# Ordering every engine's instructions by the scheduler's timeline model instead of its ordinary one

## The chip, the cores and the metric

The kernel runs on one core of a Trainium2 chip. The metric is device time in microseconds, from one run of the whole program. Times of a profiled execution come from a hardware trace of one run.

## The reference, cut to what matters

One layer of a hybrid mixer. A sequence of 2048 tokens by 1024 channels is normalized and projected, the columns are split over four mixers of width 256, each mixer runs along the sequence, and the joined result is projected back, normalized and added to the input.

```python
h = _rmsnorm(x, pre_norm_w[l])
proj = jnp.einsum('btd,de->bte', h, w_in[l])
p_gdn, p_rwkv, p_sc, p_gla = _split(proj, [GDN_COLS, RWKV_COLS, SC_COLS, GLA_COLS])
y_gdn = _gated_deltanet(...)   # chunks of 64: triangular solve, then a scan over chunks
y_rwkv = _rwkv7(...)           # a scan over tokens
y_sc = _short_conv(...)
y_gla = _gla(...)              # chunks of 64, a scan over chunks
y = jnp.concatenate([y_gdn, y_rwkv, y_sc, y_gla], axis=-1)
out = jnp.einsum('bte,ed->btd', y, w_out[l])
x = x + _rmsnorm(out, post_norm_w[l])
```

Each scan carries a state of 64x64 (GLA: 32x64) per head from chunk to chunk, four heads a mixer. RWKV is computed in chunks too, with a triangular inverse as for the gated delta rule.

## The kernel before

The sequence is cut into 4 blocks of 512 tokens, a block into 4 tiles of 128 tokens, a tile into 2 chunks of 64. All products run on TensorE (PE) through one helper line (L197) and transposes through another (L201), so a row of the profile is told apart by the tile it writes: `pp` are the projections (`proj` L476, `out_proj` L1322), `psi` the triangular inverses (`inverse` L558), `psc` the chains that carry the states (`gdn_chain` L971, `rwkv_chain` L1017, `gla` L1249), `psa` everything else (transposes, chunk matrices). Their PSUM banks are 2, 1, 2 and 3 (BANKS, L169).

Projections are in single precision split into a high and a low part (`hh`, `hl` of the activations, two halves of a tile `w` of the weights), three products each. A weight tile of 128 columns comes in two halves of 12 matmuls of 512 columns; a ring of NW = 3 halves (L161) is loaded ahead. In block 0 `load_parts` (L451) loads raw weights, splits them on ScalarE (ACT) and GpSimd (POOL) (`split`, L348) and stores the parts to DRAM; later blocks load the parts (L465). All DMAs are issued on SyncE's (SP's) queue.

An inverse works on two tiles at once: five doubling levels, each a product on `psi`, a masking on VectorE (DVE; `W`, L591), a second product, an addition (`X`, L596), a transposition and two copies; then a correction. A GDN chunk has three dependent products: state times keys, the solve (`gu<-`), the state update, with DVE or ACT between them. So inverses and chains alternate between PE and another engine, visit by visit. A norm needs a power -1/2, which POOL computes (`power`, L352, at L354).

The source decides the program order itself. Generators for chains (priority 0), inverses (1), preparation (2), outputs (3), row norms (4), late weights (5) and projections (99) are woven by `weave` (L227), which keeps a clock `t` of its own from matmul sizes, and lets projections fill until BEAT = 1.5 us of it have passed before the others get a turn:

```python
ready = [th for th in self.threads if th[0] < 99 and self.can(th)]
if main[0] == 99 and self.can(main) and (not ready or self.t - self.left < BEAT):
    self.step(main)
```

This program order isn't yet the order on the engines. When the TileContext block closes (L1431), the framework's scheduler ranks every instruction by its place in the program (`high_priority` blocks move it up by 400 places, or 4000), plays the program on a model of the chip's engines, and hands each engine of the model, when it can take one, the ready instruction of lowest rank. The lists that result are what the chip's engines run, each in its list's order, with semaphores between them. Buffers are tiles of fixed rings, so the order doesn't change which buffer an instruction uses.

## Time and profile before

| | before |
|---|---|
| median of 3 runs | 1380.93 us (1374.62 to 1382.09) |
| the profiled execution | 1382.66 us, span 1380.9 us |
| mean granted TensorE clock | 0.979 of full speed |
| busy, PE / PEld / DVE / ACT / POOL | 93% / 71% / 70% / 39% / 26% |
| moved by DMA | 204.47 MB, mean 148 GB/s |

PE is the matmul stream and PEld the weight loads, which overlap it. The span runs from the first to the last instruction. An engine's busy time is the time in which at least one of its instructions is recorded as running; a wait is put down to the instruction that released it.

### The profile page before, as it was taken

What the parts mean: (1) busy time and instruction counts of PE and PEld (TensorE: products, weight loads), DVE (VectorE), ACT (ScalarE), POOL (GpSimd) and SP (SyncE); (2) the same over time, 40 slices, a digit from 0 to 9 for tenths busy, and PEclk for the clock granted to TensorE, in tenths of its full rate; (3) what the DMA queues carried; (4) which work ended last, traced back from release to release, by engine and by line L of the source; (5) the groups of instructions that cost most, each with busy time, mean ns of one, the idle gap of its engine ahead of it and who ended that gap; (6) DMA issues with size and microseconds to landing.
All of it is one profiled execution on the core that took longest, in us unless ns stands there. A gap on an engine that the chain in (4) does not pass through costs nothing. (4 is left out here: it accounts for less than half of the span.)

```text
span 1380.9 us, 25696 instructions
## 1 busy us (share of the span) xinstructions
PE 1286.0 (93%) x9928; PEld 974.5 (71%) x9928; DVE 966.9 (70%) x2194; ACT 532.1 (39%) x1165; POOL 357.1 (26%) x437
## 2 busy tenths in 40 slices
PE   5989988899999999999999899999998998999997
PEld 3767766667767777767677677676776776777886
DVE  5776697778886787688757894888669847643222
ACT  4653454235442441435524422453234234232221
POOL 5564443301121121111311211103112144232221
PEclk9999999999999999999999999999999998999999
DMA  7876554453244424453444333532444362233442
GB/s 278 272 253 228 206 176 145 142 167 121 92 139 136 155 93 151 140 177 123 139 145 137 123 126 130 165 125 93 146 134 142 117 213 87 93 111 100 150 151 99
DMA packets 98506, 204.47 MB, mean 148 GB/s; under 512 B 9152, under 2 KB 39248, under 8 KB 98384
## 3 DMA queue, kind: packets, MB, share of 16 engines
q1 hardware_dynamic: 98384, 202.83, 44.6%
q8 instruction: 78, 1.28, 0.4%
q14 instruction: 44, 0.36, 0.1%
HBM read 153.51 MB, written 49.28 MB: 147 GB/s over the span
## 5 line engine op out<-in xcount | busy, mean ns | idle before, releaser
L197 PE MATMUL pp<-hh,w 128*128 128x512 f32 (+1 forms) x2272 | 642.2, 408 | 7.9 <-ACT hh L432 4.0
L197 PEld LDWEIGHTS pp<-hh,w 128*128 128x128 f32 (+1 forms) x2272 | 413.0, 190 | 96.8 <-issue 5.1
L197 PE MATMUL pp<-hl,w 128*128 128x512 f32 (+1 forms) x1152 | 340.7, 408 | 2.0 <-POOL hl L433 2.0
L197 PEld LDWEIGHTS pp<-hl,w 128*128 128x128 f32 (+1 forms) x1152 | 209.3, 190 | 47.3 <-POOL hl L433 3.8
L350 POOL TENSOR_TENSOR w<-raw,w 128x512 fp32r<-128x512 f32 (+1 forms) x102 | 129.2, 1270 | 222.1 <-ACT w L349 121.6
L354 POOL TENSOR_TENSOR sm<-sm,mhalf 128x4 f32<-128x4 f32 (+1 forms) x64 | 59.7, 933 | 221.7 <-DVE sm L1077 196.0
L349 ACT CAST w<-raw 128x512 fp32r<-128x512 f32 (+1 forms) x102 | 60.4, 594 | 132.2 <-issue 60.9
L197 PE MATMUL pp<-woh,w 128*128 128x512 f32 x256 | 73.8, 409 | 0.0
L659 DVE SCALAR_TENSOR_TENSOR pq<-pq,par,pq 128x512 f32<-128x512 f32 x72 | 59.0, 819 | 14.7 <-ACT pq L656 12.3
L583 DVE COPY Yb<-Y 64x512 f16<-64x512 f16 x160 | 57.2, 358 | 2.2
L197 PEld LDWEIGHTS <-Yb 128*128 128x128 f16 x640 | 24.9, 99 | 44.5 <-issue 18.7
L197 PE MATMUL psi<-W,Yb 128*128 128x64 f16 x640 | 33.1, 196 | 23.5 <-DVE W L591 16.9
L197 PEld LDWEIGHTS pp<-woh,w 128*128 128x128 f32 x256 | 48.0, 193 | 9.5
L596 DVE TENSOR_TENSOR X<-psi,X 128x512 f16<-128x512 f32 x64 | 43.9, 686 | 9.6 <-PE psi L197 9.2
L197 PEld LDWEIGHTS <-Bb 128*128 128x128 f16 x768 | 29.6, 99 | 27.2 <-issue 21.6
L1368 DVE SCALAR_TENSOR_TENSOR pq<-pq,sm,x 128x512 f32<-128x512 f32 x32 | 24.0, 751 | 31.1 <-DMA x<-in_x 20.6
L598 DVE STREAM_TRANSPOSE Y<-X 128x512 f16<-128x512 f16 x64 | 45.2, 706 | 0.9
L1357 ACT ACTIVATE x<-pp 128x512 f32<-128x512 f32 x32 | 19.1, 598 | 68.8 <-PE pp L197 68.8
L591 DVE TENSOR_TENSOR W<-psi,c 128x512 f16<-128x512 f32 x64 | 43.6, 682 | 1.7 <-PE psi L197 1.2
L197 PE MATMUL psi<-X,Bb 128*128 128x64 f16 x768 | 39.7, 195 | 4.1 <-DVE X L596 3.6
L994 ACT COPY gu<-psc 64x128 f32<-64x128 f32 x64 | 16.7, 260 | 59.0 <-PE psc L197 58.0
L1358 DVE TENSOR_TENSOR pq<-pp,lg 128x512 f32<-128x512 f32 x16 | 11.1, 691 | 36.2 <-ACT x L1357 36.2
(317 smaller groups left out, 2087.2 us busy)
## 6 DMA issues: line engine op xcount, KB each, us to landing
w<-parts SPq DMA_DIRECT2D x186, 512.0 KB, 3.3
parts<-w SPq DMA_DIRECT2D x62, 512.0 KB, 4.0
raw<-in_wt SPq DMA_DIRECT2D x62, 256.0 KB, 3.1
x<-in_x SPq DMA_DIRECT2D x56, 256.0 KB, 3.0
raw<-yd SPq DMA_DIRECT2D x32, 256.0 KB, 2.9
out<-pq SPq DMA_DIRECT2D x32, 256.0 KB, 2.1
x<-in_xt SPq DMA_DIRECT2D x24, 256.0 KB, 2.9
yd<-y SPq DMA_DIRECT2D x32, 128.0 KB, 2.0
```

The source lines that it names most:

```text
L197: return self.nc.tensor.matmul(out, w, x, **kw)
L349: self.nc.scalar.copy(hi, src)
L350: self.nc.gpsimd.tensor_tensor(lo, src, hi.bitcast(F32), ALU.subtract)
L354: self.nc.gpsimd.tensor_tensor(dst, x, self.mhalf[:, 0:x.shape[1]], ALU.pow)
L583: nc.vector.tensor_copy(Yb[hs(c), :, hs(c)], Y[hs(c)])
L591: nc.vector.tensor_tensor(W, v(ps), m4(self.lev[lv]), ALU.mult)
L596: nc.vector.tensor_tensor(X2, v(ps), X, ALU.add)
L598: nc.vector.transpose(Y, X)
L659: nc.vector.scalar_tensor_tensor(acc, p[:, i:i + BL], self.pcol("conv", 4 * ct + i), acc, ALU.mult, ALU.add)
L994: nc.scalar.copy(qh(w)[q, :, hp, :], pB[hs(hp), 0:P].rearrange("p (q d) -> p q d", q=2))
L1357: nc.scalar.activation(junk, ps[i], AF.Square, accum_out=ss[:, i:i + 1])
L1368: nc.vector.scalar_tensor_tensor(o, o, r, x, ALU.mult, ALU.add)
```

## The change

One argument of the TileContext. The program that is traced, its ranks, its tiles and its priorities are the same; the model on which the scheduler plays it is another. The framework has two models, which it calls CoreSim and TimelineSim, the second being the more detailed. So the order of the instructions on each engine can change, and the order of the DMAs on SP's queue, and nothing else.

```diff
     out = nc.dram_tensor("out_0", (S, D), F32, kind="ExternalOutput").ap()
-    with tile.TileContext(nc) as tc:
+    with tile.TileContext(nc, schedule_with_timeline_sim=True) as tc:
         K(tc, aps, out).build()
```

## Rows read from the trace of the kernel before

**Rows 1.** The page: busy us (share of the span) x instructions.

```profile
PE 1286.0 (93%) x9928; PEld 974.5 (71%) x9928; DVE 966.9 (70%) x2194; ACT 532.1 (39%) x1165; POOL 357.1 (26%) x437
```

**Rows 2.** Windows: busy us of each engine, granted clock, DMA share, GB/s.

```profile
core 0: us, PE busy (x) PEld busy (x) DVE busy (x) ACT busy (x) POOL busy (x), PEclk, DMA share, GB/s
...
595.00:880.00 285.00, 270.38 (x2289) 201.91 (x2287) 218.23 (x521) 111.94 (x249) 48.07 (x74) 1.00 0.43 139
...
0.00:310.00 310.00, 268.67 (x1798) 202.89 (x1799) 225.11 (x450) 143.83 (x293) 134.32 (x146) 0.96 0.60 207
...
310.00:1165.00 855.00, 813.13 (x6872) 611.55 (x6872) 653.78 (x1559) 336.10 (x745) 167.55 (x237) 0.99 0.42 135
...
1165.00:1381.00 216.00, 204.18 (x1260) 160.10 (x1259) 88.05 (x188) 52.18 (x127) 55.23 (x54) 0.97 0.35 116
```

**Rows 3.** Waits of PE: total us, times, longest.

```profile
PE psi L197 <- DVE W L591: 16.9, 11, 4.8
...
PE psa L201 <- POOL gs L354: 12.1, 1, 12.1
...
PE pp L197 <- DMA w<-parts: 2.4, 3, 1.2
```

**Rows 4.** Timeline around one PE stall: start us, us, then the group.

```profile
759.97 1.21 DVE L871 TENSOR_TENSOR_SCAN t<-c,t 128x512 f32<-128x512 f16 x1
...
761.12 0.67 DVE L591 TENSOR_TENSOR W<-psi,c 128x512 f16<-128x512 f32 x1
...
761.85 0.41 PE L197 MATMUL psi<-W,Yb 128*128 128x64 f16 x8 [1.75 <-DVE W L591]
...
762.09 1.39 PE L197 MATMUL pp<-hh,w 128*128 128x512 f32 x5
```

**Rows 5.** Timeline of a GDN chain in block 2.

```profile
706.16 0.60 PE L197 MATMUL psc<-Sg,kq 128*128 128x128 f32 x4
...
707.71 0.42 DVE L984 TENSOR_TENSOR gu<-gu,vT 64x256 f32<-64x256 f32 x1
...
708.52 0.45 PE L197 MATMUL psc<-gu,Yf 64*64 64x64 f32 x8
...
708.90 2.11 PE L197 MATMUL pp<-hh,w 128*128 128x512 f32 x8
...
710.94 0.45 PE L197 MATMUL psc<-gu,kT 64*64 64x64 f32 x8
```

**Rows 6.** Windows of PE alone on pp, psa, psc, psi, in that order.

```profile
595.00:880.00 285.00, 202.58 (x759) 1.00 0.43 139
595.00:880.00 285.00, 39.35 (x410) 1.00 0.43 139
595.00:880.00 285.00, 40.13 (x640) 1.00 0.43 139
595.00:880.00 285.00, 21.05 (x480) 1.00 0.43 139
```

**Rows 7.** Matmuls on psi from 595 to 880 us, two of four forms.

```profile
L197 PE MATMUL psi<-X,Bb x192: 189/193/203, 596.3 to 830.8; 128*128 128x64 f16 x192
...
L197 PE MATMUL psi<-W,Yb x160: 189/193/203, 598.5 to 828.2; 128*128 128x64 f16 x160
```

**Rows 8.** Chain that ended last, its longest step: start us, us, work, count.

```profile
1276.35 97.06 PE pp L197 x428
```

**Rows 9.** POOL's elementwise lines on the page, and a wait of DVE for POOL.

```profile
L350 POOL TENSOR_TENSOR w<-raw,w 128x512 fp32r<-128x512 f32 (+1 forms) x102 | 129.2, 1270 | 222.1 <-ACT w L349 121.6
...
L354 POOL TENSOR_TENSOR sm<-sm,mhalf 128x4 f32<-128x4 f32 (+1 forms) x64 | 59.7, 933 | 221.7 <-DVE sm L1077 196.0
...
DVE lu L1081 <- POOL sm L354: 15.1, 16, 1.9
```

**Rows 10.** SP's queue: what its weight loads wait for.

```profile
SPq L465 <- PE pp L197: 520.5, 150, 15.5
```

**Rows 11.** The page's DMA issues: count, KB each, us to landing.

```profile
raw<-in_wt SPq DMA_DIRECT2D x62, 256.0 KB, 3.1
```

## The prediction

> **What bounds the kernel now.** The page's busy table comes first: TensorE (PE) has 1286.0 us of matmul in a span of 1380.9 [rows 1], so 94.9 us of PE time is idle, and that is all that a new order of the same instructions can give back, unless the instructions themselves become shorter. The profiled execution took 1382.66 us, its span and 1.8 us around it; the median of the three timed runs is 1380.93, so a sum made against 1382.7 stands 1.7 us above the median.
>
> Next the windows show where the idle time lies [rows 2]. The first 310 us (block 0, its weights split for the first time) hold 41 us of it, the steady stretch from 310 to 1165 holds 42, the end 12. The steady stretch is three periods of 285 us, one per block; one of them has 270.4 us of PE work and 14.6 idle. The list of waits says what the idle pieces are: 12.1 us is one wait at the start, for POOL's row scale; the rest are waits of a few us, nearly all for DVE, and only 2.4 us for a weight DMA [rows 3]. The timeline of one of them shows how an order makes them: at 761.85 PE had stood 1.75 us before `psi<-W,Yb`, while the projection matmuls that follow it at 762.09 needed nothing of DVE; DVE itself was late because a scan of 1.21 us was queued ahead of `W` [rows 4]. So a position in a list is binding on this chip, and a scheduler that places a step before its operand is there costs PE that wait.
>
> The second thing to see is what the order does right. In the chain of block 2 the three steps of one chunk stand 2.36 and 2.42 us apart, with eight projection matmuls between each two; the step's DVE work ends at 708.13 and PE takes the next step at 708.52, 0.4 us later [rows 5]. This spacing is the program's own (BEAT), so here the ordinary model kept program order.
>
> **Why the spacing matters.** In one period PE has 202.6 us on `pp` and 39.4 on `psa`, 242.0 us which I call filler, and 40.1 on `psc` and 21.1 on `psi`, the recurrences [rows 6]. Inverses and chains are series: a PE visit, then DVE or ACT, then the next visit. One inverse has 12 visits (192 + 160 matmuls of two of its forms over four inverses are 6 and 5 of them, the solve's last product the twelfth) [rows 7]; four make 48. A chain tile of GDN or RWKV has 6 visits and of GLA 3, for 4 tiles each 60. Of these 108 the 12 of GLA run beside an inverse, and of the fourth inverse about half beside a chain, which leaves some 90 in series. 285 us over 90 is 3.17 us per visit: 0.45 on PE (an 8-matmul group of rows 5), 1.35 on DVE or ACT (from the end of a group at 706.76 to 708.13, 1.37), and so about 1.35 of waiting behind filler. Check: 90 x (1.35 + 1.35) = 243 us, the filler of the period. So the recurrence fills the whole period as PE does: there is no slack in it before block 3. Only the end has some: the last 428 matmuls run 97.06 us in one piece after the last chain [rows 8], more than block 3's own 192 x 0.227 = 44, so 53 us of filler is left over there.
>
> **The change, part by part.** No instruction is added, removed or altered, so the PE sum of 1286 stays, but for the clock. What moves is the place of instructions in the five lists, and DMA issues on SP's list. Three parts:
>
> (1) Stalls that better durations remove. The framework says of its two models that the ordinary one leaves out the fixed cost of GpSimd's elementwise instructions. The trace has what that is here: 64 powers of 128x4 at 933 ns and 102 subtractions at 1270 [rows 9]. PE waits little for POOL; DVE waits 15.1 us in one such place [rows 9]. The reach is the 42 us of the steady stretch and some 20 of block 0's 41 (12.1 at the start can't go, nor most of the first loads). Ends: nothing, if the new errors are as large as the old, and 62 us. I take half, 31.
>
> (2) Filler placed ahead of the recurrence. The scheduler gives an engine of the model the ready instruction of lowest rank at the moment at which that engine takes one. If the timeline model lets PE take instructions some way ahead of what the array executes, the next step of a chain isn't ready then, and ready projection matmuls of later rank go in front of it. There are always some: the weight loads wait for PE to release their buffers, 520.5 us in all [rows 10], so up to three halves of 12 matmuls, 36 x 0.227 = 8.2 us, lie ready. With k more matmuls ahead of each visit its wait is 1.35 + 0.227k. The filler of a period then lasts for 242 / (2.70 + 0.227k) visits, and each of the rest of the 90 leaves PE idle for its 1.35. k = 4: 67 visits, 31 us idle a period. k = 8: 54 and 49 us. k = 36: 22 and 92. Three periods count (block 3's R and L chains have the 53 us as cover), and the 44 us of steady idle go, since every step now finds its operand: +49, +103, +232 us. k = 0 is the lower bound, 0. No row shows k; I take k = 6, between the half and the whole of the spacing in rows 5: 242 / 4.06 = 60 visits, 30 x 1.35 x 3 = 122, less 44, +78.
>
> (3) SP's queue. The loads and stores are all issued there, in the new order. Cover: a weight load waits for PE, not PE for it (2.4 us of PE idle against 520.5 of SP's) [rows 3, 10], so I put it at nothing; without the cover, each half that comes late costs up to its landing, some 3.1 us [rows 11], and only in block 0, where DMA moves most (207 GB/s) [rows 2].
>
> Weighed against the skill: PE's weight loads are busy 202.9 + 611.6 + 160.1 us of the span in rows 2, 71%. The Trainium skill, "Perfetto Trace Analysis", section "Identifying the Most-Contended Engine", says that matmul busy time is a bad measure of TensorE's headroom and that the busy share of weight loads is one of the good ones. By it 29% of the span, some 400 us as an estimate, would be room, and a better order could win far more than part (1). The trace disagrees for the order: 428 matmuls with nothing between them still take 227 ns each [rows 8], and no order makes them denser. I give a gain beyond the 62 us of part (1) a chance of 0.01, inside B's.
>
> **Sum.** 1382.7 + 78 (part 2, with the stalls of part 1 inside it) = 1461; against the median 1460.
>
> **Rivals.**
> A, the forecast: part (2). For it: no slack in the recurrence, and filler always ready. Against it: the order of rows 5 is program order, and a model whose PE takes its next matmul only when the last is done keeps it. It decides from about two matmuls placed in front: at k = 1.6 a period has 79 visits in its filler, and the idle time of the other 11, 14.6 us, is what goes in stalls. Its times run from 1400 (k = 2.5) to 1600. Idle stretches also lower the clock: 0.96 was granted in the stretch with 41 us idle in 310, 0.99 in that with 42 in 855 [rows 2]. The Trainium skill, "TensorE: Matmul & The Clock Gate", section "HAM oscillation", has it that idle gaps send the clock down again; by that A would cost more than its idle time. The trace's two shares agree, and the sum leaves it out.
> B, the other side: the model takes instructions without running ahead, and its durations are nearer to the chip's. Half of the 62 us goes: 1382.7 - 31 = 1352. For it: nearly every PE stall of rows 3 is a step placed too early. Against it: many are a DVE queue's jitter, which no model holds. It turns into a loss if a step placed later lengthens the recurrence by over 0.5 us per visit (90 x 3 x 0.5 = 135 us of waiting, against 44 of steady idle).
> C, no change: the rank decides nearly everything and stalls only move: 1375 to 1389.
> D, a slower start alone: SP's and POOL's lists of block 0 come in a worse order and PE waits for weights there. 62 halves are split in block 0 [rows 11]; if a third are late by half a landing, 20 x 1.5 = 30 us, 1413. Against it: PE's waits there are for DVE and POOL, not DMA.
>
> **How the numbers follow.** A 0.48, D 0.07, C 0.13, B 0.32. Faster by over 0.5% is B, 0.31 with a sliver lost to C; slower is A and D but for A's smallest k, 0.55; the rest, 0.14, is within 0.5%, about what a measurement of this kernel can tell from no change. The predicted time is A's, 1460. A alone would be 1400 to 1590. Since B holds a third, the range goes down to B's middle, 1350, and up to 1580, which leaves out the best half of B's reach and k near 36.
>
> **What will show it.** A: the chain's groups of rows 5 stand further apart with more than eight `pp` matmuls between them, PE busy per period falls under 270 and there are stretches with little `pp` in which PE waits for DVE or ACT on `psc` and `psi`; the PE sum stays near 1286. B: the same spacing, and PE's waits for DVE under half of now. C: both as now. D: the windows to 310 us grow and the later periods stay at 285. The prediction is wrong if the eight matmuls between visits stay, or if more filler between them leaves PE busy all the same, which would mean that the recurrence had slack that my count of 90 doesn't see.

## The result, and the profile after

The changed kernel takes 1600.76 us (median of 4 runs, 1596.87 to 1602.41) against 1379.53 for the kernel before in runs on the same chip (4 runs): a ratio of 1.1605, 95% interval 1.1564 to 1.1645, slower. The forecast was 1460 in a range of 1350 to 1580. The direction and the place were right; the size was not.

The profiled execution took 1602.41 us with a span of 1600.6. First the page after: busy times, then the span in 40 slices of 40 us (PE's busy tenths, its granted clock in tenths, the DMA rate).

```profile
PE 1378.1 (86%) x9928; PEld 1069.5 (67%) x9928; DVE 962.9 (60%) x2194; ACT 542.8 (34%) x1171; POOL 351.9 (22%) x437
...
PE   6989987997699967996899958986899756997998
...
PEclk9999996997599977997799968995899855997999
...
GB/s 315 241 253 259 268 127 66 148 162 60 1 164 166 159 61 70 174 161 31 66 159 164 156 11 124 159 135 5 76 155 186 65 7 54 148 124 54 126 137 111
```

The matmuls are the same 9928, but the span's growth of 219.7 us over [rows 1] has two parts: PE is idle for 222.5 us where it was 94.9 (+127.6), and busy for 1378.1 where it was 1286.0 (+92.1). The slices show where: the DMA rate falls to 1, 11, 5 and 7 GB/s in single slices, and in each of these the granted clock falls to 0.5 or 0.6. A weight load is issued when PE releases a buffer, so a slice that loads nothing is one in which PE took no projection matmul.

The windows say it in numbers (busy us of each engine, granted clock, DMA share, GB/s). A window of 360 us now holds 2392 and 2372 matmuls, about 4% more than the 2289 that a period of 285 us held in [rows 2], so a period has grown to some 345 us:

```profile
0.00:310.00 310.00, 267.67 (x1604) 206.26 (x1604) 200.33 (x406) 141.39 (x281) 130.50 (x145) 0.93 0.61 211
...
395.00:755.00 360.00, 304.38 (x2392) 234.06 (x2391) 226.62 (x538) 112.14 (x247) 46.73 (x74) 0.85 0.34 112
755.00:1115.00 360.00, 306.77 (x2372) 235.99 (x2371) 235.29 (x555) 121.95 (x266) 45.78 (x74) 0.87 0.33 109
...
1115.00:1600.00 485.00, 422.01 (x2994) 332.43 (x2990) 252.69 (x583) 132.65 (x307) 117.12 (x121) 0.87 0.32 103
...
480.00:560.00 80.00, 80.00 (x539) 62.62 (x534) 32.90 (x80) 14.38 (x34) 9.13 (x13) 1.00 0.50 163
400.00:440.00 40.00, 25.34 (x299) 19.48 (x299) 35.87 (x106) 4.16 (x11) 4.31 (x6) 0.54 0.01 1
...
720.00:760.00 40.00, 25.17 (x248) 18.94 (x246) 28.18 (x68) 14.99 (x35) 2.88 (x4) 0.70 0.11 34
```

The same with PE on `pp` alone, from 480 and from 400 us:

```profile
480.00:560.00 80.00, 68.44 (x277) 1.00 0.50 163
400.00:440.00 40.00, 0.00 (x0) 0.54 0.01 1
```

So a period consists of two kinds of stretch. From 480 to 560 PE is busy for 80.00 of 80 us and does projections for 68.44 of them; from 400 to 440 it does none, and is idle for 14.7. Below is the timeline of PE in the first kind, on a GDN chain as in [rows 5] (start us, us, work, count):

```profile
523.37 0.45 PE L197 MATMUL psc<-gu,Yf 64*64 64x64 f32 x8
523.75 1.89 PE L197 MATMUL pp<-hh,w 128*128 128x512 f32 x7
525.47 1.07 PE L197 MATMUL pp<-hl,w 128*128 128x512 f32 x4
526.38 1.07 PE L197 MATMUL pp<-hh,w 128*128 128x512 f32 x4
527.38 0.32 PE L197 MATMUL psc<-gu,kT 64*64 64x64 f32 x2
...
529.48 1.20 PE L197 MATMUL pp<-hl,w 128*128 128x512 f32 x4
530.51 1.98 PE L197 MATMUL pp<-hh,w 128*128 128x512 f32 x8
532.33 1.07 PE L197 MATMUL pp<-hl,w 128*128 128x512 f32 x4
533.24 0.62 PE L197 MATMUL pp<-hh,w 128*128 128x512 f32 x2
533.69 0.60 PE L197 MATMUL psc<-Sg,kq 128*128 128x128 f32 x4
```

Between two visits of the chain stand 15 `pp` matmuls, then 18, where [rows 5] has eight. Over the whole of PE's list, 193 places between consecutive visits (`psc` or `psi`) hold three or more `pp`, with a median of 19; before, 345 did, with a median of 8. The same 3808 projection matmuls are bunched before fewer visits. The next timeline, PE and DVE in an inverse of the second kind, shows what the other visits get (in brackets the engine's idle time before, and what ended it):

```profile
734.83 0.58 PE L197 MATMUL psi<-X,Bb 128*128 128x64 f16 x8 [0.78 <-DVE X L596]
...
735.45 0.69 DVE L591 TENSOR_TENSOR W<-psi,c 128x512 f16<-128x512 f32 x1
736.06 0.58 DVE L583 COPY Yb<-Y 64x512 f16<-64x512 f16 x2
736.69 0.61 PE L197 MATMUL psi<-W,Yb 128*128 128x64 f16 x8 [1.28 <-DVE Yb L583]
...
737.34 0.69 DVE L596 TENSOR_TENSOR X<-psi,X 128x512 f16<-128x512 f32 x1 [0.70 <-PE psi L197]
738.06 0.71 DVE L598 STREAM_TRANSPOSE Y<-X 128x512 f16<-128x512 f16 x1
738.08 0.59 PE L197 MATMUL psi<-X,Bb 128*128 128x64 f16 x8 [0.78 <-DVE X L596]
```

No filler is left: PE and DVE take turns, each waiting for the other, and a group `psi<-W,Yb` of eight takes 0.61 us where it took 0.41 at full clock [rows 4]. PE's longest waits after, and the two that grew most as they were before (total us, times, longest):

```profile
PE psi L197 <- DVE Yb L583: 35.0, 19, 3.7
PE psi L197 <- DVE X L596: 21.6, 23, 3.4
PE psa L201 <- POOL gs L354: 12.1, 1, 12.1
...
PE psi L197 <- DVE W L591: 7.1, 5, 2.5
```

```profile
PE psi L197 <- DVE Yb L583: 4.3, 7, 0.9
...
PE psi L197 <- DVE X L596: 3.6, 5, 2.1
```

Against [rows 3] the wait for `W` is shorter (16.9 before), the new ones are above all for the inverse's other DVE steps, and the 12.1 for POOL is untouched. No wait of PE after is put down to a weight DMA, where it was 2.4 us.

### The profile page after: what moved, and what is told of

Read it like the earlier page. It is cut to its first block, busy times and chain, and to the rows that moved or that the text cites. A ratio compares the mean times of both kernels' runs of the same rounds, so it can differ in the third digit from the quotient of the medians.

```text
span 1600.6 us, 25731 instructions
## 1 busy us (share of the span) xinstructions
PE 1378.1 (86%) x9928; PEld 1069.5 (67%) x9928; DVE 962.9 (60%) x2194; ACT 542.8 (34%) x1171; POOL 351.9 (22%) x437
## 3 DMA queue, kind: packets, MB, share of 16 engines
q8 instruction: 78, 1.28, 0.3%
## 4 chain that ended last, share of the span: by engine, by line
PE 64%; DVE 21%; ACT 5%; DMA 4%; issue 3%; POOL 1%; SPq 0%; ACTq 0%; POOLq 0%; DVEq 0%
PE pp L197 49%; PE psc L197 7%; PE psa L197 4%; PE psa L201 2%; PE psi L197 2%; DMA x<-in_x 1%; DVE Y L598 1%; DVE X L596 1%; DVE W L591 1%; DVE Yb L583 1%; DVE hl L433 1%; DVE x L426 1%; DVE pq L659 1%; DMA parts<-w 1%; POOL sm L354 1%
## 5 line engine op out<-in xcount | busy, mean ns | idle before, releaser
L197 PE MATMUL pp<-hh,w 128*128 128x512 f32 (+1 forms) x2272 | 623.7, 403 | 12.3 <-ACT hh L432 9.3
L197 PEld LDWEIGHTS pp<-hh,w 128*128 128x128 f32 (+1 forms) x2272 | 420.2, 190 | 104.6 <-ACT hh L432 9.4
L197 PE MATMUL pp<-hl,w 128*128 128x512 f32 (+1 forms) x1152 | 334.0, 404 | 6.5 <-DVE hl L433 5.8
L197 PEld LDWEIGHTS pp<-hl,w 128*128 128x128 f32 (+1 forms) x1152 | 215.9, 191 | 57.5 <-DVE hl L433 9.2
L197 PEld LDWEIGHTS <-Bb 128*128 128x128 f16 x768 | 38.4, 110 | 55.2 <-issue 45.6
L197 PEld LDWEIGHTS <-Yb 128*128 128x128 f16 x640 | 30.1, 110 | 61.8 <-DVE Yb L583 40.7
L197 PEld LDWEIGHTS pp<-woh,w 128*128 128x128 f32 x256 | 48.1, 190 | 12.1 <-DVE pq L1358 1.3
L583 DVE COPY Yb<-Y 64x512 f16<-64x512 f16 x160 | 49.4, 308 | 1.6
L197 PE MATMUL psa<-AR,BK 64*128 64x128 f32 x256 | 43.3, 375 | 3.2 <-DVE AR L888 1.7
L1015 DVE TENSOR_TENSOR Sr<-Sr,psc 64x128 f32<-64x128 f32 x64 | 18.2, 284 | 40.7 <-PE psc L197 39.8
L197 PEld LDWEIGHTS psa<-AR,BK 64*128 64x128 f32 x256 | 36.4, 263 | 9.0 <-DVE AR L888 2.5
L792 POOL TENSOR_TENSOR t<-t,cst 128x256 f32<-128x256 f32 x16 | 12.0, 753 | 127.6 <-DVE t L791 82.0
```

What stands on the lines that cost most here:

```text
L197: return self.nc.tensor.matmul(out, w, x, **kw)
L583: nc.vector.tensor_copy(Yb[hs(c), :, hs(c)], Y[hs(c)])
L1015: self.nc.vector.tensor_tensor(sb, sb, pv[hs(hp)], ALU.add)
```

## The experiments

All of these compute the full result. The timeline model holds a constant for each engine: how many instructions it may take ahead of the one in execution, 35 for PE and 12 for the others. These are numbers of the model; whether the chip has such a thing is not claimed. **Theory:** at the moment when PE of the model takes an instruction, the next step of a recurrence isn't ready, so ready projections go in front of it, as many as the constant lets in. **Rivals:** the timeline model's ranks or readiness on the other engines do it; or any order but the program's own would.

### The dose: PE's constant at 2, 16 and 24

On the kernel after, beside the imports (the value is 2, 16 or 24):

```diff
+from concourse.hw_specs import TRN2Spec
+TRN2Spec.ENG_ISSUE_QUEUE_DEPTH[mybir.EngineType.PE] = 2
```

> The timeline model as in the change, but its constant for how many instructions PE may take ahead is set from 35 to 2; nothing else differs. Theory (PE of the model takes filler ahead, so visits of the recurrence come late): the list has 8 projection matmuls in the median between visits again, as before the change, instead of 19, so the time comes back to 1380, within 1350 to 1400, PE idle about 95 us and the granted clock about 0.98. Rival (the timeline model's durations make a worse order, on whatever engine): it stays over 1500. Rival (the other engines' lists): it stays over 1500, since they are still made on the timeline model.

> As the run with 2, but 16 instructions ahead. Its list has 12 projection matmuls in the median between visits, 4 more than before. Theory: by the prediction's formula k = 4 adds 49 us of idle time, and with the clock that the changed kernel lost (92 us beside 128 of idle, 0.72 a us) 84, so about 1465, within 1420 to 1510. Rivals: over 1550, as the changed kernel.

> The change with 24 instructions ahead on PE instead of 35. 15 projection matmuls in the median between visits, k = 7: by the formula 92 us of idle time more than before, with the clock 158, so about 1540, within 1490 to 1580. Rivals: as the changed kernel, 1600.

Measured against the kernel before (ratio, 95% interval, median time): 2 gives 0.9764 (0.9749 to 0.9778; 1342.42 us), 16 gives 1.0452 (1.0427 to 1.0476; 1437.83), 24 gives 1.1073 (1.1043 to 1.1103; 1521.38). With 35 it is 1.1605. One constant of the model, with the chip's work the same, moves the time from below the kernel before to 16% above it. The theory holds, and the loss is a matter of dose. The runs with 16 and 24 lie in their ranges; the run with 2 is 8 us faster than its range, and PE idle for 68.8 us where about 95 was expected: it does not come back to the kernel before but beats it.

### PE's list tied to program order

```diff
-        return self.nc.tensor.matmul(out, w, x, **kw)
+        return self.tc.keep_in_program_order(self.nc.tensor.matmul(out, w, x, **kw))
...
-        return self.nc.tensor.transpose(out, x, ident)
+        return self.tc.keep_in_program_order(self.nc.tensor.transpose(out, x, ident))
```

Once on the kernel after, once on the kernel before:

> The change, with every matmul and transpose tied to the one before it in the program, so that PE's list is program order; the lists of DVE, ACT, POOL and SP come from the timeline model with its own constants. Theory: the cause is PE's list alone, so 1350 to 1420. Rival (the lists of the other engines, or DMA order on SP): over 1500.

> The kernel before with PE's list tied to program order and the ordinary model for the rest: the control of the same tie on the timeline model. Theory: PE's order before was nearly program order, so 1370 to 1400. If the timeline model's durations are better for the other lists, the tied kernel on the timeline model is faster than this one by up to 2%; if not, the two agree within 0.5%.

Measured: 1.0366 (1.0336 to 1.0396; 1425.7 us) on after, 1.0593 (1.0556 to 1.063; 1455.66) on before. Tying PE to program order takes back three quarters of the loss of the change, which puts it on PE's list; the time is 6 us above its range. The second run missed its range by 56 us: the tie alone costs 6% on the kernel before, more than what is left of the loss in the first. The page and PE's first wait of that run:

```profile
PE 1304.3 (90%) x9928; PEld 995.0 (68%) x9928; DVE 975.0 (67%) x2194; ACT 533.2 (37%) x1165; POOL 356.1 (24%) x437
```

```profile
PE psi L197 <- DVE W L591: 42.9, 21, 6.1
```

The waits for `W` are 42.9 us against 16.9 in [rows 3]. So the ordinary scheduler doesn't keep program order on PE; it moves steps to where DVE has their operand. That a chain in [rows 5] shows the spacing of BEAT didn't show that the whole list is the program's. And with PE's list tied in both, the other four engines' lists of the timeline model are the better ones by 2% (1.0366 against 1.0593).

### The rivals: the other engines' constants, and the ranks

The constants of DVE, ACT, POOL and SP set to 2, PE's left at 35; then, separately, chains and inverses moved up by 4000 places in rank:

```diff
+TRN2Spec.ENG_ISSUE_QUEUE_DEPTH.update({e: 2 for e in TRN2Spec.ENG_ISSUE_QUEUE_DEPTH if e != mybir.EngineType.PE})
```

```diff
-        y = next(th[3], "end")
+        if th[0] < 2:
+            with self.tc.high_priority(offset=10 * PRIO):
+                y = next(th[3], "end")
+        else:
+            y = next(th[3], "end")
```

> The change, with the constant for instructions taken ahead set to 2 for DVE, ACT, POOL and SP (12 before), while PE keeps 35. Its PE list has 19 projection matmuls in the median between visits, as the changed kernel. Theory: it stays at about 1600, within 1540 to 1640. Rival (running ahead on the other engines delays the steps between visits): under 1500.

> The change, with everything that the generators of chains and inverses trace moved up by 4000 places in rank. Theory: a step isn't ready when the model's PE takes instructions, so its rank can't bring it forward; the list still has 19 projection matmuls in the median between visits and the time stays at 1600, within 1550 to 1650. Rival (the steps lose to filler by rank): under 1480.

Measured: 1.1583 (1.1556 to 1.1609; 1592.19 us) and 1.172 (1.1694 to 1.1746; 1611.43). Neither takes any of the loss back beyond 0.2% (the second is 1% slower than the change); the median between visits stays at 19 in both. A higher rank can't help a step that isn't ready when the engine takes its next instruction, which is what the theory says.

### The smallest dose

Constant 1 on every engine; 1 on PE alone (others 12); 2 on PE with 1 on the others:

```diff
+TRN2Spec.ENG_ISSUE_QUEUE_DEPTH.update({e: 1 for e in TRN2Spec.ENG_ISSUE_QUEUE_DEPTH})
```

> The timeline model with no engine taking more than one instruction ahead: its durations without its running ahead. Theory and my rival B: with running ahead gone the better durations are left, so PE's waits for DVE shrink by up to half and the time is 1350 to 1380. If the durations are worth nothing, 1380 to 1395.

> The change with PE's constant at 1 and the others at 12. It asks why the run with 1 on every engine took 1630 although its list has 8 projection matmuls in the median between visits. Theory: with one place the model's PE begins a matmul only when the last has left, so its matmuls are further apart than on the chip, and it finds a step ready after fewer of them than the chip needs: steps stand too early and PE waits for DVE. Then the cause is PE's 1 alone: 1560 to 1650. Rival: the 1 on DVE, ACT, POOL and SP spoils their lists; then 1335 to 1360.

> The change with PE's constant at 2 and the others at 1. By the theory of the run before this one: 1335 to 1370, as with 2 and 12 (1342). By its rival: 1560 to 1650.

Measured: 1.1844 (1.1812 to 1.1877; 1630.31 us), 1.1982 (1.1931 to 1.2033; 1649.37) and 0.9763 (0.9722 to 0.9805; 1346.45). The first was a miss of over 200 us: I had taken less as always better. The other two put it on PE's 1 alone. The page of the run with 1 on PE, and a piece of its timeline, PE and DVE:

```profile
PE 1377.5 (84%) x9928; PEld 1042.7 (63%) x9928; DVE 985.5 (60%) x2194; ACT 538.8 (33%) x1169; POOL 344.2 (21%) x437
```

```profile
603.35 0.71 PE L197 MATMUL psc<-Sg,kq 128*128 128x128 f32 x4
603.45 0.69 DVE L942 TENSOR_TENSOR M<-psa,cst 128x512 f32<-128x512 f32 x1 [1.35 <-PE psa L197]
603.82 1.18 PE L197 MATMUL pp<-hh,w 128*128 128x512 f32 x4
...
604.84 1.08 PE L197 MATMUL pp<-hl,w 128*128 128x512 f32 x4
...
605.53 1.10 DVE L946 TENSOR_TENSOR rB<-M,kn 64x128 f32<-64x128 f32 x2
...
606.65 0.42 DVE L983 TENSOR_TENSOR gu<-psc,gk 64x256 f32<-64x256 f32 x1
...
608.35 0.69 PE L197 MATMUL psc<-gu,Yf 64*64 64x64 f32 x8 [2.43 <-DVE gu L984]
```

This is another loss than that of the change. Eight `pp` stand between the visits, as they should, but DVE does preparation (`M`, `rB`) for 2.6 us after the product has ended, and takes the chain's `gu` at 606.65, so that PE stands for 2.43 us with its step already at the head of its list. In sum PE is idle for 269.2 us. Why the model with 1 on PE makes such lists was not tested; that it holds PE back too long after each matmul, and so sees DVE's steps fall due later than they do on the chip, would fit, but is only argued.

### The best dose

PE's constant at 8 with the others at 12, and 4 on every engine:

> The change with PE's constant at 8 and the others at 12: 8 projection matmuls in the median between visits. Theory: running ahead by so little is still shorter than the wait that a visit has anyway, k about 0, so 1340 to 1365; a step on the way to the 1438 of 16.

> The change with 4 on every engine, looking for the best order: 8 projection matmuls in the median between visits. Theory: 1330 to 1350, about as with 2 on PE; the constants of the other engines matter little.

Measured: 0.9683 (0.9643 to 0.9722; 1334.18 us), 6 us faster than its range, and 0.9732 (0.9694 to 0.977; 1340.3). Both are faster than the kernel before as well as the kernel after. The page of the first, and its longest waits of PE:

```profile
PE 1274.3 (95%) x9928; PEld 972.4 (73%) x9928; DVE 968.1 (72%) x2194; ACT 533.5 (40%) x1167; POOL 354.0 (26%) x437
```

```profile
PE psa L201 <- POOL gs L354: 12.7, 1, 12.7
PE psi L197 <- DVE X L579: 4.9, 4, 3.2
...
PE psi L197 <- DVE W L591: 2.7, 5, 1.5
```

Idle time is 1336.1 - 1274.3 = 61.8 us, 33 less than before. The waits for `W`, the largest in [rows 3], are down from 16.9 to 2.7 us, while POOL's one wait at the start stays. So the more detailed model does make the better order, and the run-ahead of its PE hides that. That it is its durations which make the order better was not tested apart from what else differs between the two models.

## Why the prediction was right about the place and wrong about the size

All doses in one table. Idle time is the profiled span less PE's busy time; the counts are of PE's list, places between consecutive `psc` or `psi` visits with three or more `pp`; the formula is part (2)'s, 94.9 - 44 + 3 x 1.35 x (90 - 242 / (2.70 + 0.227k)), with k, the `pp` added ahead of each visit, as the median less 8. For 1 it isn't given, since that loss is another.

| PE's constant | places, median `pp` | idle us | formula | PE busy us | clock | ratio |
|---|---|---|---|---|---|---|
| before (ordinary) | 345, 8 | 94.9 | | 1286.0 | 0.979 | 1 |
| 1 | 333, 8 | 269.2 | | 1377.5 | 0.909 | 1.1982 |
| 2 | 331, 8 | 68.8 | 52 | 1272.1 | 0.986 | 0.9764 |
| 4 (and 4 on the others) | 346, 8 | 67.1 | 52 | 1275.7 | 0.987 | 0.9732 |
| 8 | 333, 8 | 61.8 | 52 | 1274.3 | 0.990 | 0.9683 |
| 16 | 269, 12 | 112.9 | 144 | 1323.2 | 0.944 | 1.0452 |
| 24 | 228, 15 | 158.7 | 187 | 1367.9 | 0.893 | 1.1073 |
| 35 (the change) | 193, 19 | 222.5 | 227 | 1378.1 | 0.878 | 1.1605 |

**Part (2), mechanism: right.** Filler goes ahead of the next visit, runs out, and the rest of the visits leave PE idle. The stretches without `pp`, the group distances and the waits on `psi` are those that were named. Two signs of A did not come: PE busy per period was to fall under 270 us and the PE sum to stay near 1286, and both rose, for the reason of the second failed step. In the inverse from 734.83 to 738.08 us a pair of visits leaves PE idle for 0.78 + 1.28 us, 1.03 a visit, not the 1.35 of the forecast.

**Part (2), size: the first failed step is "I take k = 6".** The list has k = 11. With that the same formula gives 59 us of idle time a period; the windows, which hold a little more than a period, show 360 - 304.38 = 55.6, then 53.2, and from 1115 us to the end, with the third period in it, 485 - 422.01 = 63.0. Over the span it gives +132 instead of the forecast's +78, where +127.6 was measured. At k of 4 and 7 it is some 30 us too high and at 0 it is 10 to 17 too low, so the agreement at 11 is in part luck. The choice between the half and the whole of the spacing in [rows 5] had no row behind it; the bound of k = 36 was the honest end, and the range cut it off.

**The second failed step is the clock: "the sum leaves it out".** PE's busy time grew by 92.1 us, a term that the sum had at nothing and the larger part of the 140 us by which the forecast was low. Only two levels of the clock stand in the trace, 1 and 0.5, so a mean of 0.878 is about 390 us at the lower one, and 0.979 before was 58. By tile, PE's own busy time over the whole span went from 166.66 to 213.93 us on `psa`, from 162.54 to 193.66 on `psc` and from 85.90 to 101.28 on `psi`, together +93.8. On `pp` it fell from 1004.54 to 953.70, which longer runs of them, with fewer ends that lie beneath other work, would explain; the overlap between tiles, which the sum by tile counts twice, fell by about as much (1419.6 - 1286.0 = 133.6 before, 1462.6 - 1378.1 = 84.5 after). The two tiles that grew most, before and then after:

```profile
0.00:1700.00 1700.00, 166.66 (x1640) 0.98 0.37 120
0.00:1700.00 1700.00, 162.54 (x2560) 0.98 0.37 120
...
0.00:1700.00 1700.00, 213.93 (x1640) 0.88 0.36 120
0.00:1700.00 1700.00, 193.66 (x2560) 0.88 0.36 120
```

So the 92 us are the short matmuls, most of them in the stretches where the mean clock is 0.5 to 0.7. That it is the clock and not the lost company of other groups, the trace of the changed kernel shows for the inverse. Here a group `psi<-W,Yb` of eight stands alone, with PE idle before and after it, at full clock, and the windows give the clock there and in the group at 736.69 above:

```profile
926.01 0.41 PE L197 MATMUL psi<-W,Yb 128*128 128x64 f16 x8 [3.72 <-DVE Yb L583]
927.98 0.59 PE L197 MATMUL psi<-X,Bb 128*128 128x64 f16 x8 [1.57 <-DVE X L596]
...
926.00:926.40 0.40, 0.39 (x8) 0.32 (x9) 0.40 (x1) 0.00 (x0) 0.00 (x0) 1.00 0.00 0
736.70:737.30 0.60, 0.60 (x8) 0.49 (x9) 0.00 (x0) 0.00 (x0) 0.00 (x0) 0.50 0.00 0
```

Alone at full clock it takes the same 0.41 us as with projections right behind it in [rows 4]; alone at half the clock it takes 0.61. For the sum of 92 the case rests on two of the runs besides: the tied kernel before is idle for 150.5 us in small pieces everywhere, at a clock of 0.951, and its busy time grew by 18 us; the dose of 24 is idle for 158.7 us in stretches without filler, at 0.893, and its grew by 82. No run changed the clock alone. With k = 11 and the measured 92 the sum would have been 1382.7 + 132 + 92 = 1607, against 1602.4.

The Trainium skill, "TensorE: Matmul & The Clock Gate", section "HAM oscillation", has idle gaps send the clock down again. The windows agree (0.54 from 400 to 440 us, 1.00 from 480 to 560), and the prediction named this as a cost above the sum without giving it a number.

**Part (1), 31 us by better durations: the size came, once the run-ahead is small.** The dose of 8 has 33 us less idle time than before, and 12 less busy time at a clock of 0.990. That is rival B, and its 1352 was 18 us too high, 12 of them the busy time. The 31 was half of a reach, chosen without a row, so its nearness is luck, and durations as the reason were not tested apart. B's objection that many of the stalls are jitter of DVE's queue, which no model holds, fails for the largest of them: the waits for `W` went from 16.9 to 2.7 us. B wasn't what the change as written does.

**Part (3), SP's queue at nothing: right, and rival D fell with it.** PE's waits for weights, 2.4 us before, are gone from the list. The chains of the start are later too, but by A's mechanism: PE's idle time to 310 us is 42.3 us where it was 41.3. The windows of the changed kernel to 310 us with PE on `pp`, then on `psc`:

```profile
0.00:310.00 310.00, 220.92 (x872) 0.93 0.61 211
...
0.00:310.00 310.00, 15.19 (x224) 0.93 0.61 211
```

By then the kernel before has 838 `pp` and 332 `psc` matmuls done: with the change the projections are ahead and the chains behind.

**"Here the ordinary model kept program order": wrong for the list as a whole**, as the tied kernel before showed. It didn't move the forecast, but it was the argument against A, whose chance stood at 0.48.

**Smaller readings.** The steady idle time is 855 - 813.13 = 42 us in [rows 2], where the sum takes away 44. PE's waits of a few us are not "nearly all for DVE": of some 75 us of waits before, POOL's 12.1 aside, 58 end with DVE. The 0.55 for slower is all of A and D, with nothing off for A's smallest k. None of these moves the forecast by more than 2 us.

**No slack in the recurrence: held.** More filler between visits did leave PE idle elsewhere, in every dose above 8. At 2, 4 and 8 the spacing of the kernel before stays, and no idle time is added. The 90 itself was not counted in a trace.

## What to carry to other kernels

A scheduler that orders instructions by a model fixes its choices when the model's engine takes an instruction, so the model's run-ahead is a distance by which ready filler goes in front of a dependent step; count the filler between the visits of a recurrence in the new list before anything else, and try the model with a small run-ahead (here 2, 4 or 8, not 1) before giving it up. Where filler and recurrence both just fill a period, filler that is used early is idle time later: by the formula at k = 11, 47 visits take 47 x 11 x 0.227 = 117 us of it early, and 59 us a period are idle for that. Price that idle time with the clock: stretches without filler run the short matmuls slower as well, here 92 us beside 128 of idle time.

## What the runs showed that I had not expected

- From 400 to 440 us PE was busy for 63% of the time (25.34 of 40 us), with no wait between groups longer than 2.2 us, and was granted 0.54 of full speed: the lower of its two levels for nearly all of that stretch.
- About the same idle time cost 18 us of busy time when it lay in small pieces among projections (tied kernel before) and 82 us when it lay in stretches without them (dose 24).
- The time has a flat bottom in the dose (1342, 1340 and 1334 us at 2, 4 and 8) with a cliff on its small side: 1649 us at 1.
